# The opening of a pooling mixer: idle products on TensorE until data come, another order of loads, unsplit weights for two tiles, shorter norms

## The chip, the cores and the metric

The kernel runs on one core of a Trainium2 chip. The metric is the device time of one execution in microseconds, the median over several runs; less is better. A profile is one execution recorded by the hardware profiler; its times are microseconds from the start of the span unless marked ns. PE is TensorE (matrix products), PEld its weight loads, DVE is VectorE, ACT is ScalarE, POOL is GpSimd, SP is SyncE, which here issues all DMAs.

## The reference

One decoder layer on `x` of 1024 positions by 1024 channels, float32: a causal pooling mixer with a residual, then a gated convolutional FFN with a residual.

```python
def rms_norm(x, g):
    y = x * lax.rsqrt(jnp.mean(x * x, axis=-1, keepdims=True) + EPS)
    return y * g

def pool_mixer(x, w, b, scale):          # four groups of 256 channels, windows 2, 4, 8, 16
    for gi, w_len in enumerate(POOL_WINDOWS):
        ...                               # mean over the last w_len positions, minus x itself
        groups.append(window_sum / count - xf[..., gi * POOL_GROUP:(gi + 1) * POOL_GROUP])
    d = jnp.stack(groups, axis=2)
    y = jnp.einsum('bsgc,gcd->bsgd', d, w).reshape(bsz, seq, D_MODEL) + b
    return scale * y

def conv_ffn(x, w_in, conv_w, conv_b, w_out):
    h = causal_depthwise_conv(x @ w_in, conv_w, conv_b)
    val, gate = jnp.split(h, 2, axis=-1)
    return (jax.nn.silu(gate) * val) @ w_out

x = x + pool_mixer(rms_norm(x, norm_mix_g), pool_w, pool_b, pool_scale)
x = x + conv_ffn(rms_norm(x, norm_ffn_g), ffn_w_in, ffn_conv_w, ffn_conv_b, ffn_w_out)
```

## The kernel before

The sequence is cut into eight tiles of 128 positions, x0 to x7. The mixer takes each tile through these steps; in the profile they are known by the tiles that they write.

- `rstd_of` (lines 127 to 138): ACT squares the tile into a scratch tile, tagged `junk`, with the sum per position, and takes a square root; five operations of one column on DVE make the reciprocal root and refine it once. Its results are `st_a` for the first norm, `st_e` for the edge rows and `st_b` for the second norm. The scratch tile has one buffer in its pool.
- `mixer_norm` (L147): DVE multiplies a band matrix, which holds the windows, by that factor per position; the result is `bandr`. So the norm is put into the band and not into x.
- `mixer_window`: PE multiplies x by the band (L151, `psd`, eight F32 products that the profile shows as sixteen passes of 128 columns). The first sixteen columns of each block are completed (L196 for tile 0, L198 for the others, which adds `edges`). ACT copies the result rounded to a shorter format (`dh`, L199), and DVE takes what rounding left (`dl`, L200).
- `mixer_edges`: the sixteen rows before each tile (`x_edge`, one load with 112 rows) go through the same norm (L143) and PE (`ps_edges`), and ACT copies the result (`edges`, L169).
- `mixer_weights` (L178, L183, L184): the mixer's weights `wp_raw`, in eight blocks of 256 columns, are multiplied by the row `pool_scale`, which a DMA has broadcast to 128 partitions, and by the norm's gain; then ACT and DVE split each pair of blocks into a high part `wph` and a low part `wpl`. `mixer_bias` does the like with the bias (L158 to L162).
- `mixer_out` (L214, `psy`): 24 products of 256 columns, three for each block of channels (high by high, high by low, low by high), and two of 512 columns for the bias (L215). DVE adds x (L217), the sum goes to DRAM, and the second norm makes `diag` (L221).
- `ffn_operand` (L237, `pst`): PE transposes and scales the tile for the FFN, ACT and DVE copy and split it. The FFN's products (L303) and its output products (L576) follow, seven products in the place of eight at each of two levels.

The loop at the end of the mixer's section runs over j: it traces the norm of tile j, the window of tile j-1, the output of tile j-2 and the FFN operand of tile j-4. The program is traced in that order, and a scheduler then gives every engine its own fixed order of instructions; an engine works through its order and waits at each instruction for what that needs. `tc.issue_after(i)` puts the instructions of its block that run on the engine of `i` behind `i` in that engine's order. Pools hand out buffers by tag: a tile of a tag waits until an earlier tile's last reader has released a buffer. `ps_p` (three buffers of two PSUM banks) serves `psd`, `psy`, `ps_edges` and `pst`; `ps_x` has two buffers of one bank; the tag `raw` has two, which hold `wp_raw` and the rows first and the FFN's weights (`win`) later.

Before the change the loads are issued in this order: x0, the constants, the edge rows, `par`, the broadcast scale, x1, the weights in two loads, x2, the broadcast bias, x3 to x7.

Of the kernel before, what the change touches and what calls it, by code (L numbers as in the profile page):

```python
# [7 lines left out]
F32 = mybir.dt.float32  # L8
F32R = mybir.dt.float32r
# [5 lines left out]
P = 128  # L15
# [6 lines left out]
NG = 4  # L22
# [2 lines left out]
HALO = 16  # L25
EPS = 1e-6

CW, CB, GM = 0, 3 * 2 * NF, 4 * 2 * NF
GF = GM + NK
NPAR = GF + NK  # L30
# [3 lines left out]
BD = B0 + NG * P  # L34

NOPS_A = 3
ACT_GAIN = 7

NH = 512
# [4 lines left out]
def trunk_kernel(ctx: ExitStack, tc: tile.TileContext, x, consts, par, rows, pool_w, w_in, w_out, out):  # L44
# [16 lines left out]
    def raw_tile(name):  # L61
        return work.tile([P, 2, D], F32, tag="raw", name=name, bufs=2)
# [24 lines left out]
    def affine(t, src, op, fill, base, pattern, step):  # L87
        nc.gpsimd.affine_select(out=t, in_=src, compare_op=op, fill=fill, base=base, pattern=pattern, channel_multiplier=step)

    nc.gpsimd.memset(x_edge[:HALO, :], 0.0)  # L90
    for g, w in enumerate(WINDOWS):

        e = edge_band[:, g, :].rearrange("p (j t) -> p j t", t=HALO)
        nc.gpsimd.memset(edge_band[:, g, :], 1.0 / w)
        affine(e, e, ALU.is_gt, 0.0, w - HALO, [[-HALO, NS], [-1, HALO]], 1)
        affine(e, e, ALU.is_ge, 0.0, HALO - 1, [[HALO, NS], [0, HALO]], -1)
    for g, w in enumerate(WINDOWS):

        m = band[:, g, :]
        nc.gpsimd.memset(m, 1.0 / w)  # L100
        affine(m, m, ALU.is_ge, 0.0, 0, [[1, P]], -1)
        affine(m, m, ALU.is_gt, 0.0, w, [[-1, P]], 1)
        affine(m, m, ALU.not_equal, 1.0 / w - 1.0, 0, [[1, P]], -1)
    par_sb = const.tile([P, NPAR], F32, tag="par", name="par_sb")
    wp_raw = raw_tile("wp_raw").rearrange("p a (c d) -> p (a c) d", d=GRP)
    rows_b = raw_tile("rows_b")
    scale_b, bias_b = rows_b[:, 0, :], rows_b[:, 1, :]
    load_x(0)
    nc.sync.dma_start(cst, consts)
    nc.sync.dma_start(x_edge[HALO:, :], x.rearrange("(j r) d -> j r d", r=P)[: NS - 1, P - HALO :, :])  # L110
# [11 lines left out]
    nc.vector.memset(eps_t, EPS)  # L122
    ident = cst[:, :FAC]
    fac = cst[:, FAC:B0].rearrange("p (c t) -> p c t", t=HALO)
    band0 = cst[:, B0:].rearrange("p (g s) -> p g s", s=P)

    def rstd_of(src, name):
        junk = pp.tile([P, D], BF16, tag="junk", name=f"junk_{name}")
        st = pp.tile([P, 4], F32, tag="st", name=f"st_{name}", bufs=8)
        nc.scalar.activation(junk, src, AF.Square, accum_out=st[:, 0:1])  # L130
        nc.scalar.activation(st[:, 1:2], st[:, 0:1], AF.Sqrt, bias=eps_t, scale=1.0 / D)
        nc.vector.tensor_scalar(st[:, 0:1], st[:, 0:1], 1.0 / D, EPS, op0=ALU.mult, op1=ALU.add)
# [7 lines left out]
    bands, marks, stats = {}, {}, {}  # L140

    def edge_norm():
        nc.vector.tensor_scalar(edge_band, edge_band, rstd_of(x_edge, "e"), None, op0=ALU.mult)  # L143

    def mixer_norm(j):
        t = bands[j] = pp.tile([P, NG, P], F32, tag="bandr", name=f"bandr{j}", bufs=2)
        nc.vector.tensor_scalar(t, band if j else band0, stats[j], None, op0=ALU.mult)  # L147

    def windows(ps, src, weights):
        for c in range(NK):  # L150
            nc.tensor.matmul(ps[:, c * P : (c + 1) * P], src[:, c * P : (c + 1) * P], weights[:, c // 2, :], start=True, stop=True)  # L151


    bias_hl = pp.tile([P, D], F32R, tag="bias_hl", name="bias_hl")
    mean_w = pp.tile([P, P], F32R, tag="mean_w", name="mean_w")

    def mixer_bias():
        nc.vector.memset(mean_w.bitcast(F32), 2.0 / P)  # L158
        nc.vector.tensor_tensor(bias_b, bias_b, scale_b, ALU.mult)
        nc.scalar.activation(bias_hl, bias_b, AF.Copy)  # L160
        low = slice(P // 2, P)
        nc.vector.tensor_tensor(bias_hl[low, :], bias_b[low, :], bias_hl[low, :].bitcast(F32), ALU.subtract)  # L162

    edges = pp.tile([P, NK, P], F32, tag="edges", name="edges")

# [9 lines left out]
    def mixer_weights():  # L175
        for c in range(2 * NG):
            g = c // 2
            nc.vector.scalar_tensor_tensor(  # L178
                wp_raw[:, c, :], scale_b[:, g * GRP : (g + 1) * GRP], par_sb[:, GM + c : GM + c + 1], wp_raw[:, c, :], op0=ALU.mult, op1=ALU.mult
            )  # L180
            if c % 2:
                cs = slice(c - 1, c + 1)
                nc.scalar.activation(wph[:, cs, :], wp_raw[:, cs, :], AF.Copy)  # L183
                nc.vector.tensor_tensor(wpl[:, cs, :], wp_raw[:, cs, :], wph[:, cs, :].bitcast(F32), ALU.subtract)  # L184

    ds = {}

    def mixer_window(j):
        ps = bank2(f"psd{j}")
        windows(ps, xs[j], bands.pop(j))  # L190
        dh = pp.tile([P, NK, P], F32R, tag="dh", name=f"dh{j}", bufs=2)
        dl = pp.tile([P, NK, P], F32R, tag="dl", name=f"dl{j}", bufs=1)
        ps3 = ps.rearrange("p (c s) -> p c s", c=NK)
        first = ps3[:, :, :HALO]
        if j == 0:
            nc.vector.tensor_tensor(first, first, fac, ALU.mult)  # L196
        else:
            nc.vector.tensor_tensor(first, first, edges[:, :, j * HALO : (j + 1) * HALO], ALU.add)  # L198
        nc.scalar.activation(dh, ps3, AF.Copy)  # L199
        nc.vector.tensor_tensor(dl, ps3, dh.bitcast(F32), ALU.subtract)  # L200
        ds[j] = (dh, dl)

    n2s = {}
    x1_dram = dram.tile([S, D], F32, tag="x1_dram", name="x1_dram")

    def mixer_out(j):
        dh, dl = ds.pop(j)
        ps = bank2(f"psy{j}")
        for h in range(2):
            cols = slice(h * NH, (h + 1) * NH)  # L210
            for c in range(4 * h, 4 * h + 4):
                o = ps[:, c // 2 * GRP : (c // 2 + 1) * GRP]
                for i, (a, w) in enumerate(((dh, wph), (dh, wpl), (dl, wph))):
                    nc.tensor.matmul(o, a[:, c, :], w[:, c, :], start=c % 4 == 0 and i == 0, stop=False, skip_group_check=True)  # L214
            nc.tensor.matmul(ps[:, cols], mean_w, bias_hl[:, cols], start=False, stop=True, skip_group_check=True)  # L215
        x1 = xs.pop(j)
        marks[j] = nc.vector.tensor_tensor(x1, ps, x1, ALU.add).ins  # L217
# [3 lines left out]
        nc.vector.tensor_scalar(diag, ident, r, None, op0=ALU.mult)  # L221
        n2s[j] = (x1, diag)

    n2f = n2_pool.tile([P, NK, S], F32, tag="n2f", name="n2f")
# [380 lines left out]
def constants():  # L605

    import numpy as np

    r, t, h = np.arange(P)[:, None], np.arange(P), np.arange(HALO)
    blocks = [np.eye(P)]  # L610
    blocks += [np.tile(w / np.minimum(h + 1, w), (P, 2)) for w in WINDOWS]
    inside = [(r > t - w) & (r <= t) for w in WINDOWS]
    blocks += [(m - np.eye(P) * np.minimum(t + 1, w)) / w for m, w in zip(inside, WINDOWS)]
    return np.concatenate(blocks, axis=1).astype(np.float32)


# [32 lines left out]
```

## Time and profile before

| | |
|---|---|
| median of 3 runs | 721.1 us (720.66 to 723.61) |
| the profiled execution | 723.45 us, its span 721.7 us |
| mean granted PE clock | 0.995 |
| busy PE, PEld | 698.9 us (97%), 580.2 us (80%) |
| busy DVE, ACT, POOL | 609.7 us (84%), 352.3 us (49%), 7.7 us (1%) |
| chain that ended last | PE 80%, DVE 11%, DMA 6% |

A row of the timeline or of a group gives the start, the busy time in us, the engine, the line, the operation, output <- input, and in brackets the idle time of the engine just before it with what ended that. Rows of SPq are DMA issues. A row of the chain of waits gives start, length and what was worked on. A row of stretches gives its bounds, its length, the busy time of PE, PEld, DVE, ACT and POOL with the number of instructions, the mean granted PE clock (1.00 is full), the mean busy share of the DMA engines and the GB/s that they moved.

### The profile page before, as it was taken

How to read it: one execution, taken by the hardware profiler on the slowest of the kernel's cores; microseconds unless marked ns; L12 is line 12 of the kernel's file. 1: busy time of each engine (PE TensorE's matmuls, PEld its weight loads, DVE VectorE, ACT ScalarE, POOL GpSimd, SP SyncE). 2: the span in 40 equal slices, each digit the busy share in tenths (PEclk: the TensorE clock that was granted, in tenths of full speed). 3: DMA queues.
4: the chain of work that ended last, by engine and by line, in shares of the span. 5: the costliest groups of instructions: out<-in, count | busy, mean ns of one | idle time of the engine just before them, and what ended most of it. 6: DMA issues, size and time to landing. Idle time of an engine off the chain costs nothing.

```text
span 721.7 us, 8803 instructions
## 1 busy us (share of the span) xinstructions
PE 698.9 (97%) x3252; PEld 580.2 (80%) x3252; DVE 609.7 (84%) x941; ACT 352.3 (49%) x566; POOL 7.7 (1%) x33
## 2 busy tenths in 40 slices
PE   3799999999999999999999999999999999999997
PEld 3799977888888888888888888888888788888886
DVE  3788999999888898888888888877996998798994
ACT  4597746554444444444444444444553444344441
POOL 4000000000000000000000000000000000000000
PEclk9899999999999999999999999999999999999999
DMA  9722030222222222222122112227999910005241
GB/s 266 282 89 84 34 117 0 118 88 88 88 87 88 88 88 89 87 88 81 66 89 73 58 75 87 88 89 264 315 321 312 308 54 1 0 1 190 87 152 67
DMA packets 30881, 83.83 MB, mean 116 GB/s; under 512 B 3335, under 2 KB 4487, under 8 KB 28023
## 3 DMA queue, kind: packets, MB, share of 16 engines
q1 hardware_dynamic: 30839, 83.28, 32.8%
q8 instruction: 25, 0.41, 0.2%
q14 instruction: 17, 0.14, 0.1%
HBM read 63.34 MB, written 19.92 MB: 115 GB/s over the span
## 4 chain that ended last, share of the span: by engine, by line
PE 80%; DVE 11%; DMA 6%; issue 1%; SPq 1%; ACT 1%; DVEq 0%; ACTq 0%
PE Y L303 23%; PE oP L576 21%; PE X L303 15%; PE Z L303 15%; PE psy L214 3%; DMA blk<-g_dram 3%; PE psd L151 2%; DMA x<-in_x_dram 1%; PE pst L237 1%; DVE n2f L271 1%; DVE oBP L70 1%; DVE T L260 1%; DMA blk<-in_w_out_dram 1%; DVE blk L271 1%; DVE oAP L70 1%
## 5 line engine op out<-in xcount | busy, mean ns | idle before, releaser
L576 PE MATMUL oP<-oBP,oAP 128*128 128x512 f32 x924 | 210.8, 390 | 1.0 <-ACT oBP L69 0.6
L576 PEld LDWEIGHTS oP<-oBP,oAP 128*128 128x128 f32 x924 | 173.2, 188 | 38.5 <-DVE oBP L70 1.4
L303 PE MATMUL X<-B,A11s 128*128 128x512 f32 x264 | 65.6, 394 | 0.7 <-DVE A11s L70 0.7
L303 PE MATMUL Y<-T,S2s 128*128 128x512 f32 x264 | 65.1, 394 | 1.1 <-DVE T L260 1.0
L303 PE MATMUL Z<-B,S4s 128*128 128x512 f32 x264 | 64.1, 392 | 0.6 <-DVE r L337 0.6
L303 PE MATMUL Z<-T,S1s 128*128 128x512 f32 x264 | 64.6, 393 | 0.0
L303 PE MATMUL Y<-T,S3s 128*128 128x512 f32 x264 | 64.3, 392 | 0.0
L303 PE MATMUL Y<-T,A22s 128*128 128x512 f32 x264 | 64.1, 392 | 0.0
L303 PE MATMUL X<-B,A12s 128*128 128x512 f32 x264 | 63.4, 390 | 0.0
L303 PEld LDWEIGHTS Y<-T,S2s 128*128 128x128 f32 x264 | 49.2, 188 | 13.2 <-DVE T L260 1.5
L303 PEld LDWEIGHTS X<-B,A11s 128*128 128x128 f32 x264 | 49.3, 188 | 12.3 <-DVE A11s L70 1.1
L303 PEld LDWEIGHTS Z<-B,S4s 128*128 128x128 f32 x264 | 49.5, 188 | 11.8 <-issue 1.1
L303 PEld LDWEIGHTS Z<-T,S1s 128*128 128x128 f32 x264 | 49.5, 188 | 11.4 <-ACT S1s L69 0.2
L303 PEld LDWEIGHTS Y<-T,S3s 128*128 128x128 f32 x264 | 49.6, 188 | 11.2
L303 PEld LDWEIGHTS Y<-T,A22s 128*128 128x128 f32 x264 | 49.5, 188 | 11.1 <-ACT val L350 0.3
L303 PEld LDWEIGHTS X<-B,A12s 128*128 128x128 f32 x264 | 49.5, 188 | 10.3
L361 ACT ACTIVATE gate<-gate 128x1024 f32<-128x1024 f32 x22 | 23.4, 1061 | 43.5 <-DVE gate L352 43.5
L69 ACT ACTIVATE oBP<-blk 128x512 fp32r<-128x512 f32 x32 | 20.2, 633 | 46.9 <-PE oP L576 41.6
L351 DVE SCALAR_TENSOR_TENSOR val<-ha,par_sb,val 128x1023 f32<-128x1023 f32 x22 | 28.2, 1282 | 12.5 <-ACT val L350 12.5
L343 DVE TENSOR_TENSOR ha<-Z,q 128x512 f32<-128x512 f32 x20 | 13.8, 691 | 23.9 <-PE Z L303 23.9
L69 ACT ACTIVATE S4s<-win 128x512 fp32r<-128x512 f32 x22 | 13.9, 633 | 40.4 <-PE Z L303 35.9
L350 ACT ACTIVATE gate<-hb,par_sb 128x1024 f32<-128x1024 f32 x22 | 27.4, 1245 | 11.9 <-DVE hb L345 11.9
(130 smaller groups left out, 1094.2 us busy)
## 6 DMA issues: line engine op xcount, KB each, us to landing
win<-in_w_in_dram SPq DMA_DIRECT2D x22, 1024.0 KB, 4.8
g_dram<-val SPq DMA_DIRECT2D x22, 512.0 KB, 2.6
blk<-g_dram SPq DMA_DIRECT2D x33, 256.0 KB, 5.4
blk<-in_w_out_dram SPq DMA_DIRECT2D x31, 256.0 KB, 5.5
A12s<-g_dram SPq DMA_DIRECT2D x22, 256.0 KB, 5.0
B21s<-in_w_out_dram SPq DMA_DIRECT2D x22, 256.0 KB, 3.5
x<-in_x_dram SPq DMA_DIRECT2D x8, 512.0 KB, 10.4
x_dram<-x SPq DMA_DIRECT2D x8, 512.0 KB, 2.6
```

The costliest lines, as they stand in the source:

```text
L69: nc.scalar.activation(t[:, 0, :], src, AF.Copy)
L70: nc.vector.tensor_tensor(t[:, 1, :], src, t[:, 0, :].bitcast(F32), ALU.subtract)
L151: nc.tensor.matmul(ps[:, c * P : (c + 1) * P], src[:, c * P : (c + 1) * P], weights[:, c // 2, :], start=True, stop=True)
L214: nc.tensor.matmul(o, a[:, c, :], w[:, c, :], start=c % 4 == 0 and i == 0, stop=False, skip_group_check=True)
L237: nc.tensor.matmul(ps[:, c * P : (c + 1) * P], x1[:, c * P : (c + 1) * P], diag, start=True, stop=True)
L271: nc.vector.tensor_tensor(out, a, b, ALU.subtract)
L303: nc.tensor.matmul(bank, a[:, i, ks], b[:, l, k, :], start=opens and m == 0, stop=m == 11, skip_group_check=not opens)
L343: tt(hid[n, "a"][:, NH:], bank, hid[n, "q2"], ALU.add)
L350: nc.scalar.activation(t, src, AF.Identity, bias=par_sb[:, CB + f : CB + f + 1], scale=w[2])
L351: nc.vector.scalar_tensor_tensor(t[:, 1:], src[:, : S - 1], w[1], t[:, 1:], op0=ALU.mult, op1=ALU.add)
L361: nc.scalar.activation(gate, gate, AF.Silu)
L576: nc.tensor.matmul(obanks[set_, i], a[:, u, i * P : (i + 1) * P], b[:, v, :], start=opens and g == 0 and m == 0, stop=g == NP2 - 1 and m = ...
```

## The change

PE multiplies a tile of zeros by itself before data come (`keep_warm`): eight products of 512 columns in bf16, then the two products that broadcast the scale row into PSUM, then two more. The rows are loaded first, one as a single row and both on eight partitions; the bias is multiplied and split there and moved to two partitions by two small DMAs, and the bias products take a weight of two rows of ones. The edge rows come in seven DMAs of sixteen rows, behind x1. A square root on a constant is run early. The norm takes three DVE operations of one column, and its two factors are applied in one operation; the constant `FOLD` goes into the bands and the identity. Tiles 0 and 1 are multiplied by the unsplit F32 weights with one product for each block of channels; the split of the weights moves behind the edge norm. The edges are traced behind the window of tile 1.

```diff
+WHOLE = 2
...
+    idle = pp.tile([P, NH], BF16, tag="junk", name="idle")
+    nc.vector.memset(idle, 0.0)
+    idle_ps = bank2("idle_ps")[:, :NH]
+    def keep_warm(n):
+        for _ in range(n):
+            nc.tensor.matmul(idle_ps, idle[:, :P], idle, start=True, stop=True)
+    keep_warm(8)
+    nc.sync.dma_start(row_sb, rows[:1, :])
+    nc.sync.dma_start(rows8, rows.rearrange("r (k p) -> k r p", p=P))
     load_x(0)
     nc.sync.dma_start(cst, consts)
-    nc.sync.dma_start(x_edge[HALO:, :], x.rearrange("(j r) d -> j r d", r=P)[: NS - 1, P - HALO :, :])
     nc.sync.dma_start(par_sb, par)
-    nc.sync.dma_start(scale_b, rows[:1, :].to_broadcast([P, D]))
-    load_x(1)
     for g in range(0, NG, 2):
         nc.sync.dma_start(wp_raw[:, 2 * g : 2 * g + 4, :], pool_w[g : g + 2].rearrange("g (k p) d -> p (g k) d", p=P))
-    load_x(2)
-    nc.sync.dma_start(bias_b, rows[1:, :].to_broadcast([P, D]))
-    for j in range(3, NS):
+    b8 = rows8[:, 1, :]
+    nc.vector.tensor_tensor(b8, b8, rows8[:, 0, :], ALU.mult)
+    nc.scalar.activation(bias8[:, 0, :], b8, AF.Copy)
+    nc.vector.tensor_tensor(bias8[:, 1, :], b8, bias8[:, 0, :].bitcast(F32), ALU.subtract)
+    for l in range(2):
+        nc.sync.dma_start(bias_hl[l : l + 1, :].bitcast(F32), bias8[:, l, :].bitcast(F32))
+    load_x(1)
+    for j in range(NS - 1):
+        nc.sync.dma_start(x_edge[HALO * (j + 1) : HALO * (j + 2), :], x[(j + 1) * P - HALO : (j + 1) * P, :])
+    for j in range(2, NS):
         load_x(j)
...
+    warm = pp.tile([P, 1], F32, tag="warm", name="warm")
+    nc.scalar.activation(warm, eps_t, AF.Sqrt)
...
-        nc.scalar.activation(st[:, 1:2], st[:, 0:1], AF.Sqrt, bias=eps_t, scale=1.0 / D)
-        nc.vector.tensor_scalar(st[:, 0:1], st[:, 0:1], 1.0 / D, EPS, op0=ALU.mult, op1=ALU.add)
-        nc.vector.reciprocal(st[:, 2:3], st[:, 1:2])
-        nc.vector.scalar_tensor_tensor(st[:, 3:4], st[:, 2:3], st[:, 0:1], st[:, 2:3], op0=ALU.mult, op1=ALU.mult)
-        nc.vector.tensor_scalar(st[:, 3:4], st[:, 3:4], -0.5, 1.5, op0=ALU.mult, op1=ALU.add)
-        nc.vector.tensor_tensor(st[:, 2:3], st[:, 2:3], st[:, 3:4], ALU.mult)
-        return st[:, 2:3]
+        marks[name] = nc.scalar.activation(st[:, 1:2], st[:, 0:1], AF.Sqrt, bias=eps_t).ins
+        nc.vector.tensor_scalar(st[:, 0:1], st[:, 0:1], D * EPS, None, op0=ALU.add)
+        nc.vector.scalar_tensor_tensor(st[:, 3:4], st[:, 1:2], st[:, 1:2], st[:, 0:1], op0=ALU.mult, op1=ALU.add)
+        nc.vector.reciprocal(st[:, 2:3], st[:, 3:4])
+        return st[:, 1:2], st[:, 2:3]
+    def normed(out, src, r):
+        return nc.vector.tensor_scalar(out, src, r[0], r[1], op0=ALU.mult, op1=ALU.mult).ins
...
+    ones = pp.tile([2, P], F32R, tag="ones", name="ones")
+    nc.vector.memset(ones.bitcast(F32), 1.0)
+    scale_b = []
+    for h in range(2):
+        t = ps_x.tile([P, NH], F32, tag="X", name=f"scale{h}")
+        nc.tensor.matmul(t, ones[:1, :].bitcast(F32), row_sb[:, h * NH : (h + 1) * NH], start=True, stop=True)
+        scale_b += [t[:, :GRP], t[:, GRP:]]
+    keep_warm(2)
...
+        if j < WHOLE:
+            dh = dh.bitcast(F32)
+            marks[f"whole{j}"] = nc.scalar.activation(dh, ps3, AF.Copy).ins
+            ds[j] = [(dh, wp_raw)]
+            return
...
+        ds[j] = [(dh, wph), (dh, wpl), (dl, wph)]
...
-                for i, (a, w) in enumerate(((dh, wph), (dh, wpl), (dl, wph))):
+                for i, (a, w) in enumerate(terms):
...
         if j == 0:
+            stat(1)
             edge_norm()
-            stat(1)
         if 0 <= j - 1 < NS:
             mixer_window(j - 1)
+        if j == 0:
+            mixer_weights(range(4))
         if j == 1:
-            mixer_edges()
-            mixer_weights()
-            mixer_bias()
-        if 0 <= j - 2 < NS:
+            with tc.issue_after(marks["first"]):
+                mixer_weights(range(4, 8))
+            with tc.issue_after(marks["edge"]):
+                mixer_out(0)
+        if 1 <= j - 2 < NS:
             mixer_out(j - 2)
+        if j == 2:
+            with tc.issue_after(marks["edge"]), tc.issue_after(marks["e"]):
+                split_weights()
```

`marks["first"]` is the first-column product of tile 0 (L196), `marks["edge"]` the edge norm on DVE (L143), `marks["e"]` the square root of the edge norm on ACT. `split_weights` is the copy and the subtraction of L183 and L184 for all four pairs of blocks; `mixer_edges` is called in `mixer_window(1)` behind its window products.

More of the change, by code (lines that the diff above doesn't have):

```diff
@@ L26 @@
 EPS = 1e-6
+FOLD = 2 * D**0.5
 CW, CB, GM = 0, 3 * 2 * NF, 4 * 2 * NF
@@ L93, in trunk_kernel @@
         e = edge_band[:, g, :].rearrange("p (j t) -> p j t", t=HALO)
-        nc.gpsimd.memset(edge_band[:, g, :], 1.0 / w)
+        nc.gpsimd.memset(edge_band[:, g, :], FOLD / w)
         affine(e, e, ALU.is_gt, 0.0, w - HALO, [[-HALO, NS], [-1, HALO]], 1)
@@ L99, in trunk_kernel @@
         m = band[:, g, :]
-        nc.gpsimd.memset(m, 1.0 / w)
+        nc.gpsimd.memset(m, FOLD / w)
         affine(m, m, ALU.is_ge, 0.0, 0, [[1, P]], -1)
         affine(m, m, ALU.is_gt, 0.0, w, [[-1, P]], 1)
-        affine(m, m, ALU.not_equal, 1.0 / w - 1.0, 0, [[1, P]], -1)
+        affine(m, m, ALU.not_equal, FOLD / w - FOLD, 0, [[1, P]], -1)
     par_sb = const.tile([P, NPAR], F32, tag="par", name="par_sb")
     wp_raw = raw_tile("wp_raw").rearrange("p a (c d) -> p (a c) d", d=GRP)
-    rows_b = raw_tile("rows_b")
@@ L107, in trunk_kernel @@
-    scale_b, bias_b = rows_b[:, 0, :], rows_b[:, 1, :]
+    rows_raw = raw_tile("rows_raw")
+    row_sb = rows_raw[:1, 0, :]
+    rows8, bias8 = (rows_raw[:NK, 1, i * NH : i * NH + 2 * P].rearrange("k (r p) -> k r p", p=P) for i in range(2))
+    bias8 = bias8.bitcast(F32R)
+    bias_hl = pp.tile([2, D], F32R, tag="bias_hl", name="bias_hl")
+    idle = pp.tile([P, NH], BF16, tag="junk", name="idle")
[4 more added lines that the diff above has]
+            nc.tensor.matmul(idle_ps, idle[:, :P], idle, start=True, stop=True)
@@ L119, in trunk_kernel @@
+    for j in range(2, NS):
         load_x(j)
     eps_t = const.tile([P, 1], F32, tag="eps", name="eps_t")
-    nc.vector.memset(eps_t, EPS)
+    nc.vector.memset(eps_t, D * EPS)
+    warm = pp.tile([P, 1], F32, tag="warm", name="warm")
+    nc.scalar.activation(warm, eps_t, AF.Sqrt)
     ident = cst[:, :FAC]
@@ L125, in trunk_kernel @@
     band0 = cst[:, B0:].rearrange("p (g s) -> p g s", s=P)
+    marks = {}
     def rstd_of(src, name):
@@ L151, in windows @@
             nc.tensor.matmul(ps[:, c * P : (c + 1) * P], src[:, c * P : (c + 1) * P], weights[:, c // 2, :], start=True, stop=True)
[L154 to L162, printed above, removed]
+    ones = pp.tile([2, P], F32R, tag="ones", name="ones")
[6 more added lines that the diff above has]
+    keep_warm(2)
     edges = pp.tile([P, NK, P], F32, tag="edges", name="edges")
@@ L173, in trunk_kernel, with mixer_weights, split_weights @@
     wpl = pp.tile([P, 2 * NG, GRP], F32R, tag="wpl", name="wpl")
-    def mixer_weights():
-        for c in range(2 * NG):
-            g = c // 2
+    def mixer_weights(cs):
+        for c in cs:
             nc.vector.scalar_tensor_tensor(
-                wp_raw[:, c, :], scale_b[:, g * GRP : (g + 1) * GRP], par_sb[:, GM + c : GM + c + 1], wp_raw[:, c, :], op0=ALU.mult, op1=ALU.mult
+                wp_raw[:, c, :], scale_b[c // 2], par_sb[:, GM + c : GM + c + 1], wp_raw[:, c, :], op0=ALU.mult, op1=ALU.mult
             )
[L181 to L184, printed above, removed]
+    def split_weights():
+        for c in range(0, 2 * NG, 2):
+            cs = slice(c, c + 2)
+            nc.scalar.activation(wph[:, cs, :], wp_raw[:, cs, :], AF.Copy)
+            nc.vector.tensor_tensor(wpl[:, cs, :], wp_raw[:, cs, :], wph[:, cs, :].bitcast(F32), ALU.subtract)
     ds = {}
@@ L190, in mixer_window @@
         windows(ps, xs[j], bands.pop(j))
+        if j == 1:
+            mixer_edges()
         dh = pp.tile([P, NK, P], F32R, tag="dh", name=f"dh{j}", bufs=2)
-        dl = pp.tile([P, NK, P], F32R, tag="dl", name=f"dl{j}", bufs=1)
         ps3 = ps.rearrange("p (c s) -> p c s", c=NK)
@@ L195, in mixer_window @@
         if j == 0:
-            nc.vector.tensor_tensor(first, first, fac, ALU.mult)
+            marks["first"] = nc.vector.tensor_tensor(first, first, fac, ALU.mult).ins
         else:
             nc.vector.tensor_tensor(first, first, edges[:, :, j * HALO : (j + 1) * HALO], ALU.add)
+        if j < WHOLE:
[3 more added lines that the diff above has]
+            return
+        dl = pp.tile([P, NK, P], F32R, tag="dl", name=f"dl{j}", bufs=1)
         nc.scalar.activation(dh, ps3, AF.Copy)
         nc.vector.tensor_tensor(dl, ps3, dh.bitcast(F32), ALU.subtract)
-        ds[j] = (dh, dl)
+        ds[j] = [(dh, wph), (dh, wpl), (dl, wph)]
     n2s = {}
@@ L206, in mixer_out @@
     def mixer_out(j):
-        dh, dl = ds.pop(j)
+        terms = ds.pop(j)
         ps = bank2(f"psy{j}")
@@ L212, in mixer_out @@
                 o = ps[:, c // 2 * GRP : (c // 2 + 1) * GRP]
-                for i, (a, w) in enumerate(((dh, wph), (dh, wpl), (dl, wph))):
+                for i, (a, w) in enumerate(terms):
                     nc.tensor.matmul(o, a[:, c, :], w[:, c, :], start=c % 4 == 0 and i == 0, stop=False, skip_group_check=True)
-            nc.tensor.matmul(ps[:, cols], mean_w, bias_hl[:, cols], start=False, stop=True, skip_group_check=True)
+            nc.tensor.matmul(ps[:, cols], ones, bias_hl[:, cols], start=False, stop=True, skip_group_check=True)
         x1 = xs.pop(j)
@@ L220, in mixer_out @@
         diag = pp.tile([P, P], F32, tag="diag", name=f"diag{j}", bufs=2)
-        nc.vector.tensor_scalar(diag, ident, r, None, op0=ALU.mult)
+        normed(diag, ident, r)
         n2s[j] = (x1, diag)
@@ L609, in constants @@
     r, t, h = np.arange(P)[:, None], np.arange(P), np.arange(HALO)
-    blocks = [np.eye(P)]
+    blocks = [np.eye(P) * FOLD]
     blocks += [np.tile(w / np.minimum(h + 1, w), (P, 2)) for w in WINDOWS]
     inside = [(r > t - w) & (r <= t) for w in WINDOWS]
-    blocks += [(m - np.eye(P) * np.minimum(t + 1, w)) / w for m, w in zip(inside, WINDOWS)]
+    blocks += [(m - np.eye(P) * np.minimum(t + 1, w)) / w * FOLD for m, w in zip(inside, WINDOWS)]
     return np.concatenate(blocks, axis=1).astype(np.float32)
```

6 lines of the change are left out of this document (3 added, 3 removed).

## The prediction

> **What bounds the kernel now.** I read the page first, then the chain of waits in order of time, then the busy time of each engine in stretches cut where that chain changes, and last the timeline of the opening.
>
> ```profile
> span 721.7 us, 8803 instructions
> PE 698.9 (97%) x3252; PEld 580.2 (80%) x3252; DVE 609.7 (84%) x941; ACT 352.3 (49%) x566; POOL 7.7 (1%) x33
> ...
> 30.19 1.24 DVE dl L200
> 31.46 1.70 PE psy L214 x12
> 33.16 0.23 PE psy L215
> 33.40 1.44 PE psy L214 x12
> 34.84 0.24 PE psy L215
> 35.07 1.78 PE psd L151 x16
> ...
> 75.75 1.23 DVE x L217
> ...
> 111.88 2.56 PE X L303 x10
> ...
> 0.00:31.46 31.46, 16.01 (x90) 14.78 (x90) 16.28 (x51) 15.78 (x25) 7.68 (x33) 0.89 0.90 292
> 31.46:75.48 44.02, 44.02 (x354) 42.94 (x355) 36.51 (x106) 35.86 (x88) 0.00 (x0) 1.00 0.22 88
> 32.58:54.70 22.12, 22.12 (x185) 21.78 (x185) 17.71 (x60) 21.52 (x50) 0.00 (x0) 1.00 0.24 97
> 75.48:111.88 36.40, 34.01 (x171) 27.87 (x170) 36.13 (x57) 23.27 (x48) 0.00 (x0) 1.00 0.20 73
> ```
>
> In the stretches the columns after the length are busy PE, PEld, DVE, ACT, POOL, then the granted clock, the DMA share and GB/s. From 31.46, the first matmul of psy1, PE has no gap for 44.02 us; then DVE is full for 36 us; from 111.88 it is PE again. All three stretches hang on what went before, so they start earlier if psy1 does. Before 31.46 PE worked 16.01 us of 31.46. The question is therefore when psy1 can start, with psd0 to psd2, the edges and psy0 behind it, as now.
>
> **The opening, row by row.**
>
> ```profile
> 0.81 0.38 SPq L81 DMA_DIRECT2D x<-in_x_dram  x1
> 0.93 0.17 DVE L158 MEMSET mean_w<- 128x128 f32 x1
> 1.70 0.99 SPq L110 DMA_DIRECT2D x_edge<-in_x_dram  x1
> 4.21 1.06 ACT L130 ACTIVATE junk_a<-x 128x1024 bf16<-128x1024 f32 x1 [2.13 <-DMA x<-in_x_dram]
> 5.38 1.28 ACT L131 ACT_TABLE_LOAD   x1
> 7.00 0.15 DVE L132 TENSOR_SCALAR st_a<-st_a 128x1 f32<-128x1 f32 x1 [5.90 <-ACT st_a L131]
> 8.12 0.49 DVE L147 TENSOR_SCALAR bandr<-cst,st_a 128x512 f32<-128x512 f32 x1
> 8.66 3.40 PE L151 MATMUL psd<-bandr,x 128*128 128x128 f32 x16 [8.66 <-DVE bandr L147]
> 11.40 1.06 ACT L130 ACTIVATE junk_e<-x_edge 128x1024 bf16<-128x1024 f32 x1 [4.44 <-DMA x_edge<-in_x_dram]
> 14.06 1.06 ACT L130 ACTIVATE junk_a<-x 128x1024 bf16<-128x1024 f32 x1 [1.18 <-DMA x<-in_x_dram]
> 16.73 0.63 ACT L183 ACTIVATE wph<-wp_raw 128x512 fp32r<-128x512 f32 x1 [0.29 <-DVE wp_raw L178]
> 17.80 1.02 ACT L169 ACTIVATE edges<-ps_edges 128x1024 f32<-128x1024 f32 x1 [0.44 <-PE ps_edges L151]
> 18.67 0.68 DVE L184 TENSOR_TENSOR wpl<-wp_raw,wph 128x512 fp32r<-128x512 f32 x1
> 18.81 2.05 PE L151 MATMUL psd<-bandr,x 128*128 128x128 f32 x16 [1.04 <-DVE bandr L147]
> 19.27 1.66 DVE L178 SCALAR_TENSOR_TENSOR wp_raw<-rows_b,par_sb,wp_raw 128x256 f32<-128x256 f32 x4
> 26.65 0.29 DVE L198 TENSOR_TENSOR psd<-psd,edges 128x128 f32<-128x128 f32 x1
> 26.98 1.02 ACT L199 ACTIVATE dh<-psd 128x1024 fp32r<-128x1024 f32 x1 [1.83 <-DVE psd L198]
> ...
> 14.42:17.77 3.35, 3.35 (x16) 3.05 (x16) 2.36 (x10) 2.62 (x5) 0.00 (x0) 0.58 1.05 393
> 22.56:25.22 2.66, 0.00 (x1) 0.00 (x0) 2.66 (x8) 1.87 (x3) 0.00 (x0) 0.99 0.54 214
> 25.22:28.16 2.94, 2.94 (x13) 2.94 (x14) 2.21 (x6) 1.02 (x1) 0.00 (x0) 0.50 0.76 283
> ```
>
> Two things delay the opening: data and DVE work ahead of the tiles, and a half clock. Sixteen passes of a window product take 1.78 us at full clock (35.07) and 3.40 at 8.66; in the edges' stretch from 14.42 the granted clock is 0.58, and after the idle 2.66 us from 22.56 it is 0.50.
>
> **The change, part by part.**
>
> *Zero tile on PE.* The tile `idle` bears the tag "junk" in a pool with one buffer, the buffer into which the Square of every norm writes. So the Square of x0 waits for the last of the ten idle products, and these have the two scale products between them. DVE's first memset ends near 1.1; take PE from 1.2. A pass of 128 columns of the F32 products takes 1.78 / 16 = 0.111 us, and two passes make a product, each at two column times; 512 columns in one plain pass then cost about 0.22 at full clock (the X products' 2.56 / 10 = 0.26 is the nearest row), 0.44 at half. Eight: 3.5 us at half, 1.8 at full. A scale product is F32, 512 columns in two passes: 8 x 0.111 = 0.89, twice that at half; the pair 1.8 to 3.6. The last two idle products: 0.4 to 0.9. psd0 ran at half clock for all its 3.40 us, so I let the clock rise after about 3.5 to 5 us of work: E, the end of the idle work, is 1.2 + 3.5 + 2.2 + 0.5 = 7.4. Its bounds are 1.2 + 1.8 + 1.8 + 0.4 = 5.2 and 1.2 + 3.5 + 3.6 + 0.9 = 9.2. x0 itself, behind two small row loads of 0.4 us of issue each, lands near 4.2 + 0.9 = 5.1: it is E that is late next, not x0.
>
> *Norm.* From Square to psd0 now takes 8.66 - 4.21 = 4.45 us. The second table load goes from the path (1.28; the early Sqrt on eps_t loads it while ACT waits anyhow). Five tiny operations (7.00 to 8.12) become three: about 0.7, since each dependent one takes some 0.2 and 0.3 lies ahead of the band product, which takes its two factors in one instruction as L132 does now: 0.4 saved. So 2.75: psd0 starts at 7.4 + 2.75 = 10.15, 1.5 later than now.
>
> *psd0.* PE idles 2.75 us after the idle products. The nearest row is the 2.66 us at 22.56, after which the clock is 0.50; so I take the half clock again: 3.40, to 13.55. At full clock it would be 1.78.
>
> *Whole weights.* psd0 needs the first-column product (0.29) and one copy (1.02), 1.4 with the hand-overs as at 26.65; the low half (1.24, as at 30.19) is gone for tiles 0 and 1, and psy0 no longer waits for a split weight. psy0 starts at 14.95. Its cost: eight F32 products of 256 columns, 8 x 4 x 0.111 = 3.55 plus two bias products of 0.24, together 4.0; now 1.70 + 1.44 + 0.47 = 3.6 at the most, 3.4 usually, so about 0.65 more for each of the two tiles. Scaling the eight weight blocks (0.4 each) lies on DVE while psd0 and the copy run; without that cover the second four would cost 1.6.
>
> *PE after that.* psy0 to 18.95, then psd1, edges and psd2 at 1.78 each: 20.7, 22.5, 24.3. psy1 waits behind the edges for the edge copy (1.02), the first columns (0.29) and its own copy (1.02), 2.4 in all: 22.5 + 2.4 = 24.9, with psd2 beneath. psy1 starts 31.46 - 24.9 = 6.55 earlier, and lasts 0.65 longer: 5.9.
>
> *Loads.*
>
> ```profile
> SPq L81 <- DMA wp_raw<-in_pool_w_dram: 1.2, 1, 1.2
> ...
> x_dram<-x SPq DMA_DIRECT2D x8, 512.0 KB, 2.6
> ```
>
> PE asks for psd1 at 18.95, for the edges at 20.7, for psd2 at 22.5; less 2.75 each, x1 is needed by 16.2, the edge rows by 17.95, x2 by 19.75. Now x1 lands at 14.04 and the edge rows at 11.4. The queue of SP now takes row loads, x0, consts, par, two weight loads, the two small bias moves, x1, seven edge issues and x2: at some 0.45 each x1 is issued near 5.4, the last edge piece near 9.0, x2 behind it, a little later where SP waits for an earlier load to land, as it does for 1.2 us in the row of waits above. The two broadcasts (1 MB) are gone. Were the edges to need 9.7 us from their last issue, as the one load does now (1.70 to 11.40), they would come at 18.7, 0.75 late; were all as quick as x0 (3.4), 5 us early. I take nothing, and keep 0 to 0.75.
>
> *Bias and splits.* The bias becomes three operations of 128 columns on 8 partitions instead of three over 1024 columns, none of it on the new path. The weights' splits (ACT 4 x 0.63, DVE 4 x 0.68) move behind the edge norm; psy2 alone asks for them, near 24.9 + 4.0 + 1.78 = 30.7. DVE between 10 and 25 has some 10 us of work left. Zero, and up to 2.5 if they fall into ACT's full stretch (21.52 of 22.12 us from 32.58).
>
> *Norms later.* Two tiny operations fewer each lie beside PE until 75.48; in DVE's full stretch only the last tile's norm is left: 0.2 saved.
>
> Sum: 5.9 + 0.2 = 6.1 us. The profiled execution took 723.45 (span 721.7 and 1.75 around it): 717.3. It lies 2.35 above the median of the runs; against that median, 721.1 - 6.1 = **715.0**.
>
> **The rivals.**
>
> (a) The clock holds through the gap. Then psd0 takes 1.78: 7.7 us saved, 713.4; with E at its low bound, 2.2 more, 711.2. Against it stands the 0.50 after 2.66 us of idleness; for it, that after the 1.04 us before 18.81 sixteen passes took only 2.05, so a gap is not always punished. The Trainium skill, TensorE: Matmul & The Clock Gate, "Why this matters for your kernels", allows idle gaps up to about 3 us without a drop; by that rule this case, 713.4, would be the forecast. The trace's 2.66 us disagrees.
>
> (b) Late clock: E at 9.2 (1.8 later) and psy0 at half clock for its first 3 us too (1.5): 2.8 us saved, 718.3.
>
> (c) The splits return in ACT's or DVE's full stretch: 6.1 - 2.5 = 3.6, 717.5.
>
> (d) The seven edge loads run one behind the other. A 512 KB store lands in 2.6 us (the row under *Loads*); seven times that from 5.9 is 24.1, 6.1 after the edges are needed: 721.1, no change. Against it: loads issued 0.4 us apart land together now. The Trainium skill, DMA: Bandwidth & Descriptors, "Rules for kernel authors", says of many small transfers to make one large one, as below 64 KB one pays mostly overhead; no run here shows such small ones yet.
>
> (e) Slower: SP is held by the bias moves. They stand in its queue before x1, the edges and x2 and wait for a copy on ACT and a subtraction on DVE. From the bias to the last edge landing are 10 issues of 0.45 and 3.4 us, 7.9. The gain is gone when the edges land at 24.05, so when the bias comes at 16.15; a subtraction queued on DVE behind the first columns (13.85) and four weight blocks comes at 15.5, one queued behind anything later makes the kernel slower, by as much as it is later: at 19.9, 724.8. Its row load is tiny and among the first, so it should be ready near 4.3.
>
> **How the numbers follow.** Chances: forecast 0.47, (a) 0.20, (b) 0.12, (c) 0.12, (d) 0.05, (e) 0.04. A difference below 0.5%, 3.6 us, can't be told from none here. Faster: the first two, half of (b) and a little over half of (c), 0.80; same: the rest of these and (d), 0.16; slower 0.04. The range runs from (a) with a low E, 711.2, to (b) with the 0.4 that separates runs: 718.7; (d), (e) and a tail of (c) lie outside.
>
> **What would show it.** E near 7.4 and the Square of x0 right behind the last idle product, waiting for PE; psd0 at 10.1 with sixteen passes in 3.4 us; psy0 near 15 in 4.0; psy1 near 24.9; then 44.7 gapless us of PE. I am wrong if x1 or the edges land after 18, if DVE holds back a band, or if gaps appear on PE between psy1 and 70.

## The result: slower by 0.7%, and the profile after

The kernel after takes **727.11 us** (725.94 to 728.14, five runs), the kernel before 721.78 (720.66 to 723.61) in the same comparison: a ratio of 1.0071 with a 95% interval of 1.0050 to 1.0091. 715.0 was forecast. The profiled execution of after took 727.39, its span 4.0 longer than before's. First the page, then the busy time in stretches cut where the chain changes, as before:

```profile
span 725.7 us, 8781 instructions
PE 711.5 (98%) x3250; PEld 581.2 (80%) x3250; DVE 605.6 (83%) x906; ACT 350.8 (48%) x566; POOL 7.8 (1%) x33
...
29.27:79.25 49.98, 49.98 (x347) 43.53 (x347) 34.67 (x78) 33.77 (x83) 0.00 (x0) 1.00 0.22 85
79.25:115.37 36.12, 33.92 (x171) 27.93 (x171) 36.12 (x55) 23.35 (x48) 0.00 (x0) 1.00 0.20 74
115.37:725.70 610.33, 605.32 (x2638) 494.42 (x2638) 520.53 (x729) 277.84 (x405) 0.00 (x0) 1.00 0.31 112
```

psy1 starts 2.19 us earlier than before (29.27 against 31.46). Then PE is gapless to the end of psy7, for 49.98 us. In before that stretch is 44.27 and not the 44.02 of the prediction's row, which is cut where psy7's last bias product begins; this row of before's chain of waits shows it:

```profile
75.48 0.25 PE psy L215
```

So PE needs 5.7 us more. DVE's stretch, from the end of psy7 to the FFN's next products, takes 36.13 before and 36.12 after. The remaining 610.33 is 0.5 longer than before's 721.7 - 111.88 = 609.8. Together: 4.0 us later. So two things are to be explained: why an always busy PE needs 5.7 us more for the same seven tiles, and why psy1 starts at 29.27 and not at 24.9.

**The gapless stretch.** The chain of waits of after in this stretch, tile 2:

```profile
36.01 1.43 PE psy L250 x12
37.44 0.42 PE psy L251
37.86 1.62 PE psy L250 x12
39.49 0.42 PE psy L251
39.91 1.98 PE pst L273 x16
41.89 1.79 PE psd L180 x16
```

A bias product (L251) takes 0.42, before 0.23 to 0.24. What follows one is longer too: the second twelve products take 1.62, the first 1.43; sixteen passes behind a bias product 1.98, the sixteen after those 1.79. Per tile this is 2 x 0.19 + 0.19 + 0.19 = 0.76; for seven tiles, the last of which has no passes behind it in the stretch, 5.1. The timeline of the weight loads shows where it arises, first in before, then in after:

```profile
34.56 0.19 PEld L215 LDWEIGHTS psy<-bias_hl,mean_w 128*128 128x128 f32 x1
```

```profile
33.54 0.18 PEld L251 LDWEIGHTS psy<-bias_hl,ones 2*128 2x128 f32 x1 [0.33 <-issue]
33.96 1.86 PEld L180 LDWEIGHTS psd<-bandr,x 128*128 128x128 f32 x16 [0.24 <-issue]
```

The brackets are the idle time of the load path ahead of the load. Before has none: the bias's weight has 128 rows like its neighbours', and each load goes on beneath the running product. In after the load with two rows waits 0.33 and the next one with 128 rows waits 0.24 (these rows are of psy1; behind the split products of the later tiles the first wait is 0.14). The unsplit products of psy1 add 0.6 to the 5.1 (29.27 to the end of its second bias product at 34.03 are 4.76, before 31.46 to 35.07 are 3.61, and 0.57 of the 1.15 between them is the bias). That makes the 5.7.

**The opening.** The chain of waits of after up to psy1; `idle_ps` are the idle products:

```profile
1.25 3.59 PE idle_ps L123 x8
4.85 2.15 PE scale L188 x4
7.00 0.55 PE idle_ps L123 x2
7.58 1.16 ACT junk_a L158 x2
...
10.32 3.79 PE psd L180 x16
...
15.55 3.66 PE psy L250 x8
19.21 0.42 PE psy L251
19.63 1.93 PE psy L250 x8
21.56 0.44 PE psy L251
...
29.27 1.99 PE psy L250 x8
```

The idle work ends at 7.55, x0's Square follows, psd0 runs at half clock, and psy0 takes 6.45 (15.55 to 22.00): its first eight products 3.66, where the same eight of psy1 take 1.99.

### The profile page after: what moved, and what is told of

Same layout as the page of the kernel before. It is cut to its first block, busy times and chain, and to the rows that moved or that the text cites. A ratio compares the mean times of both kernels' runs of the same rounds, so it can differ in the third digit from the quotient of the medians.

```text
span 725.7 us, 8781 instructions
## 1 busy us (share of the span) xinstructions
PE 711.5 (98%) x3250; PEld 581.2 (80%) x3250; DVE 605.6 (83%) x906; ACT 350.8 (48%) x566; POOL 7.8 (1%) x33
## 4 chain that ended last, share of the span: by engine, by line
PE 81%; DVE 10%; DMA 5%; ACT 2%; issue 1%; SPq 1%; DVEq 0%; ACTq 0%
PE Y L339 22%; PE oP L618 21%; PE X L339 15%; PE Z L339 14%; PE psy L250 4%; DMA blk<-g_dram 2%; PE psd L180 2%; DMA B21s<-in_w_out_dram 2%; PE pst L273 1%; DVE T L296 1%; DVE oBP L74 1%; DVE n2f L307 1%; PE psy L251 1%; DMA blk<-in_w_out_dram 1%; DVE blk L307 1%
```

## The experiments

Theory A: the two-row weight costs about 0.76 us per tile because loads of another number of rows can't be prepared beneath running products. Its rivals: reading a bias that lies on two partitions is slow, or the whole weights (the unsplit ones of tiles 0 and 1) cost more than thought. Theory B: the shared scratch buffer and the clock cost what the opening lost.

**e1, the bias on 128 rows again.** After, with zeros under the two rows of the bias and ones in all rows of its weight.

```diff
-    bias_hl = pp.tile([2, D], F32R, tag="bias_hl", name="bias_hl")
+    bias_hl = pp.tile([P, D], F32R, tag="bias_hl", name="bias_hl")
+    nc.gpsimd.memset(bias_hl.bitcast(F32), 0.0)
...
-    ones = pp.tile([2, P], F32R, tag="ones", name="ones")
+    ones = pp.tile([P, P], F32R, tag="ones", name="ones")
```

> The changed kernel with its bias products taken over 128 rows (126 of them zero) and a weight of 128 rows of ones. Theory A: the weight of two rows is what costs, because neither it nor the full weight behind it is loaded beneath running products; each of 16 bias products then costs 0.39 us too much (0.42 against 0.24 for itself, 0.19 more for the twelve products behind it), 6.1 us in all: 727.1 - 6.1 = 721.0. In the trace a bias product goes back to 0.24 and the second twelve to 1.44. Rival B: the late and half-clocked opening (psy1 at 29.3, psy0 in 6.45 us) is the cause: no change, 727.

Measured: 721.45 us (717.93 to 722.87), ratio to before 0.9984 (0.9970 to 0.9998), 5.7 less than after. The chain of waits, and the row of the timeline that opens the last stretch (111.88 in before, 115.37 in after):

```profile
36.53 1.43 PE psy L251 x12
37.96 0.24 PE psy L252
38.20 1.42 PE psy L251 x12
39.62 0.23 PE psy L252
39.85 1.78 PE pst L274 x16
...
111.60 2.57 PE L340 MATMUL X<-B,A11s 128*128 128x512 f32 x10 [0.68 <-DVE A11s L74]
```

Every price is back: 0.24, 1.42, 1.78, and in the timeline no idle time of the load path stands at the bias's weight any more. From psy1 to the end of psy7 PE takes 44.9 us, 0.6 more than in before, as the unsplit products cost. From psy1 (30.56 in this execution) to the last stretch there are 81.0 us, in after 86.1, in before 80.4.

**e2 and e3, the kernel before with 2 rows and with 64 rows.** The bias product reads the first rows only; the edit of e2 stands here, and e3 has 64 in place of 2.

```diff
-        nc.vector.memset(mean_w.bitcast(F32), 2.0 / P)
+        nc.vector.memset(mean_w.bitcast(F32), 1.0 / 2)
...
-            nc.tensor.matmul(ps[:, cols], mean_w, bias_hl[:, cols], start=False, stop=True, skip_group_check=True)
+            nc.tensor.matmul(ps[:, cols], mean_w[:2, :], bias_hl[:2, cols], start=False, stop=True, skip_group_check=True)
```

> The kernel before with its bias products taken over the first two of the 128 rows only (weight 1/2; the low part of the bias is left out). Theory A: 7 tiles in the stretch that PE fills, 0.75 us each, and a little for tile 0: 721.8 + 5.5 = 727.3. Rival B: no change, 721.8.

> The kernel before with its bias products taken over the first 64 rows (weight 1/64; the low part of the bias is left out). Theory A, with any change in the number of rows of a weight as the cause: as with two rows, 727.3. Rival C, the product is slow because its operand lies on two partitions: no change, 721.8.

Measured: e2 728.61 us (726.12 to 730.40), ratio 1.0088 (1.0069 to 1.0107); e3 727.52 (726.30 to 729.14), ratio 1.0076 (1.0063 to 1.0090). The loads of e3:

```profile
33.42 0.18 PEld L215 LDWEIGHTS psy<-bias_hl,mean_w 64*128 64x128 f32 x1
33.84 0.19 PEld L214 LDWEIGHTS psy<-wph,dh 128*128 128x128 f32 x1 [0.24 <-issue]
```

So this edit makes the kernel before as slow as after, and the times with 64 rows and with two can't be told apart: what costs is a weight with fewer rows than its neighbours', not the reading of two partitions. Theory A stands, and its rivals fall. The Trainium skill, TensorE: Matmul & The Clock Gate, "The mechanism", says that a weight load overlaps with running products only when its row group differs; the same section also names a background weight buffer as the other way. Here loads on the same 128 rows are the ones that overlap, and those on 64 or 2 of these rows wait; the measurement decides against the "only".

**e4, another buffer for the idle tile,** and nothing else. It takes the buffer of `dl`, which nothing needs until psy2.

```diff
-    idle = pp.tile([P, NH], BF16, tag="junk", name="idle")
+    idle = pp.tile([P, NH], BF16, tag="dl", name="idle")
```

> The changed kernel with the zero tile in the buffer of the low part dl, which is free until tile 2, in place of the buffer of the norm's scratch tile. Theory A2: the first Square starts when x0 lands, near 5.1 in place of 7.58; psd0 follows the idle products within 0.4 us and runs at full clock (1.8 in place of 3.8), as does psy0: psy1 about 5 us earlier, 727.1 - 5 = 722. Rival: the clock falls all the same: 2.4 saved, 724.7; or x1 and the edges, which land late, hold psd1 and psy1 where they are: 1 to 2 saved, 725.5.

Measured: 723.06 us (721.39 to 724.96), 4.0 less than after; ratio 1.0012 (0.9996 to 1.0027). Rows of its timeline:

```profile
4.96 1.06 ACT L158 ACTIVATE junk_a<-x 128x1024 bf16<-128x1024 f32 x1 [1.53 <-DMA x<-in_x_dram]
7.73 3.68 PE L180 MATMUL psd<-bandr,x 128*128 128x128 f32 x16 [0.59 <-DVE bandr L167]
12.86 1.99 PE L250 MATMUL psy<-wp_raw,dh 128*128 128x256 f32 x8 [1.45 <-ACT dh L231]
```

x0's Square now waits for x0's load and not for PE. psd0 starts 2.6 earlier, still at half clock although PE idles 0.59 before it; psy0's first half is at full speed. The shared buffer cost some 4 us.

**e5, e1 and e4 together.**

> The changed kernel with both edits: bias products over 128 rows and the zero tile in its own buffer. If the two costs add up: 727.1 - 5.65 - 4.05 = 717.4. If they overlap (the wait for the scratch tile was partly hidden by what the bias cost): 719 to 721.

Measured: 717.61 us (715.97 to 721.63), ratio 0.9939 (0.9917 to 0.9961). The two costs add: 727.11 - 5.7 - 4.0 = 717.4. In this execution the last stretch opens here:

```profile
108.17 2.56 PE L340 MATMUL X<-B,A11s 128*128 128x512 f32 x10 [0.69 <-DVE A11s L74]
```

**e6, the scale product over 128 rows,** the row padded with zeros and loaded behind x0; otherwise e5. On PE all ten idle products now come ahead of the scale passes.

```diff
...
-        nc.tensor.matmul(t, ones[:1, :].bitcast(F32), row_sb[:, h * NH : (h + 1) * NH], start=True, stop=True)
+        nc.tensor.matmul(t, ones.bitcast(F32), row_sb[:, h * NH : (h + 1) * NH], start=True, stop=True)
```

> As e5_both, with the two products that broadcast the scale row taken over 128 rows too (127 of them zero; the row load goes behind x0). Theory D: products over one row keep PE busy in the trace but do not count for its clock, and the clock falls at 7.6 because they filled the time before: now the clock, once up, stays at 1.00 through psd0 (1.8 us in place of 3.7) and psy1 comes up to 2 us earlier: 715.5. Rival: zeros don't count either, or the moment at which the clock rises is chance: psd0 again in 3.4 to 3.8 us, 717.4.

Measured: 717.25 us (716.28 to 718.23), ratio 0.9937 (0.9921 to 0.9953). The timeline:

```profile
6.59 7.03 SPq L143 DMA_DIRECT2D x_edge<-in_x_dram  x7
7.29 2.05 PE L182 MATMUL psd<-bandr,x 128*128 128x128 f32 x16 [0.66 <-DVE bandr L169]
10.07 1.66 DVE L207 SCALAR_TENSOR_TENSOR wp_raw<-scale,par_sb,wp_raw 128x256 f32<-128x256 f32 x4 [2.83 <-DMA wp_raw<-in_pool_w_dram]
14.63 1.06 ACT L160 ACTIVATE junk_a<-x 128x1024 bf16<-128x1024 f32 x1 [1.64 <-DMA x<-in_x_dram]
```

psd0 is at full speed (2.05, in e4 3.68 behind a gap of the same length), as expected; but the time is that of e5. psd0 isn't the bound any more: DVE waits for the weights' load until 10.07, and psd0's first columns (11.64) stand behind their scaling in DVE's order, so psy0 starts at 13.04 only, behind 3.70 us of idleness and slower again (2.69 for its first eight products). ACT waits for x1's load until 14.63, SP is 7.03 us in issuing the seven edge loads, and psy1 starts at 26.30, in e5 at 27.24.

**e7, no idle products at all;** otherwise e1.

```diff
-        for _ in range(n):
+        for _ in range(0):
             nc.tensor.matmul(idle_ps, idle[:, :P], idle, start=True, stop=True)
```

> The changed kernel with bias products over 128 rows and without the ten idle products. The Square of x0 starts when x0 lands or when the scale products end. If the idle products bring nothing (psd0 runs at half clock with them too), this equals e5_both, 717.4. If they help, psd0 and psy0 are at half clock here and not there: 719 to 720. If they only cost, through the buffer, it is faster than the 721.45 of e1_bias_128_rows by 3 to 4 us.

Measured: 719.27 us (716.81 to 721.80), ratio 0.9960 (0.9945 to 0.9974). It beats e1 by 2.2, as x0's Square no longer waits for PE; against e5 it is 1.7 slower by the medians, but the intervals overlap, so whether the idle products are worth anything is not settled. In its chain of waits the edge rows are late:

```profile
11.27 3.29 DMA x_edge<-in_x_dram
...
14.62 1.16 ACT junk_e L159 x2
```

**e8, split weights for all tiles** (`WHOLE = 0`, the splits straight behind the weights), otherwise e5.

```diff
-WHOLE = 2
+WHOLE = 0
...
                 mixer_weights(range(4, 8))
+            split_weights()
...
-        if j == 2:
-            with tc.issue_after(marks["edge"]), tc.issue_after(marks["e"]):
-                split_weights()
```

> As e5_both, with no whole weights: all tiles use split weights, and the splits stand right behind the scaling. PE saves 0.65 us for each of two tiles (1.3), but 2.5 us on ACT, 2.7 on DVE and two low parts of 1.2 on DVE come back ahead of psy0 and psy1. Theory (as in the prediction): psy1 comes 3 to 4 us later, net 2 to 3 us slower than e5_both, 720. Rival: those splits lie beneath the wait for x1 and the edges: 1 us faster, 716.4.

Measured: 721.68 us (720.01 to 723.50), ratio 1.0000 (0.9988 to 1.0013). The whole weights are worth 4.1 us to e5. psy0 waits for the low half of the split:

```profile
15.20 0.48 PE L251 MATMUL psy<-wpl,dh 128*128 128x256 f32 x1 [1.85 <-DVE wpl L214]
```

**e9, the norms of tiles 3 and 4 behind tile 1's copy on ACT,** otherwise e5. In after two Squares of later tiles stand in ACT's order ahead of what psy1 waits for, the edge copy and tile 1's copy:

```profile
25.04 1.04 ACT L158 ACTIVATE junk_a<-x 128x1024 bf16<-128x1024 f32 x1
...
26.08 1.00 ACT L197 ACTIVATE edges<-ps_edges 128x1024 f32<-128x1024 f32 x1
...
27.17 1.04 ACT L158 ACTIVATE junk_a<-x 128x1024 bf16<-128x1024 f32 x1
...
28.21 1.00 ACT L231 ACTIVATE dh<-psd 128x1024 f32<-128x1024 f32 x1
```

```diff
-        stat(j + 2)
+        if j not in (1, 2):
+            stat(j + 2)
+        if j == 2:
+            with tc.issue_after(marks["whole1"]):
+                stat(3)
+                stat(4)
         stat(j + 1)
```

> As e5_both, with the norms of tiles 3 and 4 queued on ACT behind the whole copy of tile 1. If the two Squares of 1.04 us each that stand before the edge copy and before that copy are what held psy1 from 25.7 (the end of the edges, 23.4, and 2.4 behind them) to 27.2: psy1 1 to 1.5 us earlier, 717.6 - 1.2 = 716.4. Rival: the later tiles' norms come too late instead and psd3 waits: 717.6 or slower.

Measured: 716.93 us (716.24 to 718.25), ratio 0.9924 (0.9900 to 0.9947); the time can't be told apart from e5's. psy1 starts at 23.46, 3.8 earlier than in e5, but the last stretch only 2.0 earlier (the first row is of the chain of waits, the others of the timeline):

```profile
23.46 2.00 PE psy L251 x8
```

```profile
34.89 0.63 ACT L73 ACTIVATE A11s<-win 128x512 fp32r<-128x512 f32 x1 [1.67 <-DMA win<-in_w_in_dram]
...
106.19 2.56 PE L340 MATMUL X<-B,A11s 128*128 128x512 f32 x10 [0.67 <-DVE A11s L74]
```

The FFN's first weights come into the buffer of `wp_raw`, which whole products read until psy1 ends; ACT waits for them until 34.89, and its queue is late behind that. Most of the 3.8 isn't the edit's. The profiled execution of e5 had slow scale products (the row of its timeline below) and a slow psy0 (3.38 for its first eight products):

```profile
4.78 3.78 PE L189 MATMUL scale<-rows_raw,ones 1*128 1x512 f32 x4
```

In e9's the same took 1.98 and 2.00, and the edges ended 3.1 earlier. From the end of the edges to psy1 there are 3.7 us in e5 and 3.0 in e9: by these two executions the order is worth 0.7.

**e10 and e11, the edge loads issued by ACT,** with e9's order; e10 on e6, e11 on e7.

```diff
-        nc.sync.dma_start(x_edge[HALO * (j + 1) : HALO * (j + 2), :], x[(j + 1) * P - HALO : (j + 1) * P, :])
+        nc.scalar.dma_start(x_edge[HALO * (j + 1) : HALO * (j + 2), :], x[(j + 1) * P - HALO : (j + 1) * P, :])
```

> As e6_scale_128_rows, with the order of e9 and the seven edge loads issued from ACT's queue in place of SP's, where they waited for earlier loads (4.1 us for the weights). If these waits bind the opening of e6 (the edges' Square at 16.1, x1's at 14.6): x_edge before 11, psy1 near 23.5 in place of 26.3: 717.25 - 3 = 714.3. Rival: the loads still wait for one another, whatever queue issues them: 716 to 717.

> As e7_no_idle (no idle products), with the order of e9 and the edge loads on ACT's queue. If the edges' wait was the bound there (Square of the edges at 14.6): 719.3 - 2 = 717. Against e10: the difference, 2 to 3 us by theory D, is what the full clock at psd0 and psy0 is worth; none, if the idle products bring nothing.

Measured: e10 724.63 us (723.82 to 725.55), ratio 1.0030 (1.0015 to 1.0046); e11 725.78 (724.32 to 728.52), ratio 1.0050 (1.0032 to 1.0067). Both expectations fell. ACT in e10:

```profile
5.04 3.65 ACTq L143 DMA_DIRECT2D x_edge<-in_x_dram  x3
8.72 1.28 ACT L150 ACT_TABLE_LOAD   x1 [4.67 <-DMA par_sb<-in_par_dram]
...
10.12 1.04 ACT L160 ACTIVATE junk_a<-x 128x1024 bf16<-128x1024 f32 x1
```

Issuing three edge loads held ACT for 3.65 us, with the table load and x0's Square behind them: the Square comes at 10.12, in e6 at 4.46. Between e10 and e11, 2 to 3 us were expected if the full clock is worth something; there are 1.2, and the intervals overlap.

**e12, whole weights for tile 0 alone** (`WHOLE = 1`), otherwise e9.

> The kernel of e9 with whole weights for tile 0 alone; tile 1 uses the split weights, and the norms of tiles 3 and 4 stand on ACT behind tile 1's rounded copy. Theory A (in e9 the whole weights keep the raw weights' buffer until psy1 ends, so the FFN's first weights are issued at 27.5 and land at 34.89, and ACT's queue gives back most of the 3.8 us that psy1 gained): the buffer comes free when the splits are read, near 22, the FFN's weights land before 30, ACT waits for them no longer, psy1 starts near 24.7 (a subtraction of 1.23 on DVE is added), and the time is 714.0 to 716.0. Rival B: the subtraction and the splits delay psy1 and PE's next groups by more than the earlier load saves, as e8 showed for both tiles (4.1 us lost): 717 to 719. The bias, the idle tile's buffer and all else are as in e9.

Measured: 716.91 us (715.38 to 719.66), ratio 0.9918 (0.9900 to 0.9936): no different from e9. The FFN's weights come in time, but psy1 waits for the subtraction that tile 1 needs again:

```profile
29.15 0.39 PE L251 MATMUL psy<-wph,dl 128*128 128x256 f32 x1 [0.84 <-DVE dl L237]
...
31.16 0.62 ACT L73 ACTIVATE A11s<-win 128x512 fp32r<-128x512 f32 x1
```

Gain and loss seem to cancel, and the time lies between the two expectations; this profile is of the slowest of the six executions, with the scale products at 3.78 again. e5, e6, e9 and e12 all beat the kernel before by 0.6 to 0.8%, and are not told apart from one another.

## Why the prediction was wrong, step by step

The step that failed is the bias. "Two bias products of 0.24" carried over a duration from products with a weight of 128 rows to products with two, and "none of it on the new path" looked at the operations that make the bias and not at the product that uses it, fourteen times in the gapless stretch, where each 0.2 us counts in full. 44.7 us were forecast there, 44.9 with the 0.25 that the forecast's row leaves out, and 49.98 came; e1, with the weight mended, took 44.9. No rival named it; the chance of 0.04 for slower stood on a wait of SP's queue instead. e1 takes 5.7 us away by this alone, and e2 puts 6.5 into the kernel before.

With the bias mended, 721.45 still lies 6.4 above the forecast. That is the opening, where the forecast had psy1 at 24.9; it came at 29.27 in after and at 30.56 in e1. In after:

- **Idle work to 7.4:** 7.55, and x0's Square waited for it. The wait was forecast and left standing as a fixed term; e4 shows that it was worth 4 us.
- **Norm in 2.75:** 2.77, from 7.55 to 10.32. **psd0 at half clock in 3.40:** 3.79 from 10.32, with the granted clock 0.50 in the second row below:

```profile
7.55:10.32 2.77, 0.00 (x0) 0.00 (x0) 1.13 (x5) 1.44 (x3) 0.84 (x4) 0.71 1.02 371
10.32:14.12 3.80, 3.78 (x16) 3.49 (x16) 1.56 (x4) 0.00 (x0) 0.00 (x0) 0.50 0.35 97
```

  Rival (a), the clock that holds, fell. The rule weighed there, of the Trainium skill, TensorE: Matmul & The Clock Gate, "Why this matters for your kernels", is not borne out: this gap of 2.77 us lies under its 3 us, and the clock was half. That the gap halved it is not shown, as e4 has half clock behind 0.59 us.
- **psy0 at 14.95 in 4.0:** at 15.55 in 6.45. The first half at half clock cost 1.9 more and the bias products and what follows them about 0.55. Rival (b) had the half clock in psy0, at 1.5. E at 9.2, its other part, did not come in this execution, but did in e1: the scale products there took 3.78 instead of 2.15, E was 9.5, and psd0 started at 12.31.
- **psy1 2.4 after the edges:** the edges ended at 25.75 and psy1 came at 29.27, 3.5 later. The 1.1 more lie in ACT's queue, with the two Squares shown at e9 (of which e9 got 0.7 back); the sum had counted ACT's operations on the path and not the order of its queue. So psy1's 4.4 us are 3.05 at the end of psy0, 0.2 in the passes behind it, and 1.1 here.
- **Loads, zero to 0.75:** in after PE waited for none. SP, though, was held longer than forecast by loads that had not landed, with x2 issued at 13.69 only, and e6 and e7 show that the loads are the next bound once the opening is quicker:

```profile
SPq L141 <- DMA wp_raw<-in_pool_w_dram: 3.0, 2, 1.8
```

- **Splits at nothing, whole products 0.65 a tile:** right: ACT's splits end by 25, and psy1's whole products are 0.6 longer. **Norm 0.2:** not seen, as DVE's full stretch takes 36.13 before and 36.12 after. Rivals (c), (d) and (e) did not come.

The rest of the idea was worth a good part of what was forecast: with the weight and the buffer mended, e5 takes 717.61 us, 4.1 less than the kernel before in the same comparison, and e9, with ACT's order mended too, 716.93, 5.0 less; 6.1 were forecast. That both lie inside the range given (711.2 to 718.7) does not bear out the sum: in their profiled executions psy1 starts at 27.24 and 23.46, and not at 24.9.

## What to carry to other kernels

A product's price belongs to its neighbours as well: a weight with fewer rows among weights of 128 saved no time here and cost some 0.4 us in a busy PE, so pad small weights with zeros, and count a changed operand once for every instruction that reads it. A buffer shared by tag ties its first user to its second, and a filler task must share with nothing that is on the path. Before a gain in an opening is added up, read the queue orders of the engines behind it: what stands ahead of the awaited instruction, and which load or buffer is late next.

## What the runs showed of the hardware that was not expected

- A weight load with another number of rows than its neighbours' (2 or 64 against 128) isn't prepared beneath running products: the load path idles 0.14 to 0.33 us ahead of it and 0.24 behind it, and each such product costs about 0.38 us (after, e2, e3).
- psd0 took 3.68 us at half clock in e4, 0.59 us behind eight idle products, four passes over one row and two idle products; in e6 2.05, 0.66 us behind ten idle products and four passes over 128 rows. In e8 and e9, with passes over one row too, psd0 took 3.4 and 3.7 behind gaps of 0.66 and 0.51. That passes over one row don't keep the clock up is the likely reading, with a single profile on the other side, and there the order on PE differs too.
- The clock's rise isn't the same from one execution to the next: behind the same eight idle products (3.59 us) the four scale passes took 2.15 us in after and 3.78 in e1, with the same instructions on PE up to there; e8 and e9 are like after (2.12, 1.98), e5 and e12 like e1 (3.78). This is read from the durations: the granted clock is recorded as 1.00 there in both kinds of execution.
- Issuing DMAs can hold the issuing engine while earlier loads are under way: the seven issues on SP in e6 took 7.0 us, 4.1 of them in two waits for the weights' loads. Three on ACT in e10 took 3.65, where the profile ends ACT's wait with the landing of `par`.
